# One block of scores for the second query block of the sliding attention, merged by a predicated copy

## The chip, the cores and the metric

The kernel runs on one core of a Trainium2 chip. The metric is the device time of one execution in microseconds, median over several runs. The core has TensorE (PE, with its weight loads PEld), VectorE (DVE), ScalarE (ACT), GpSimd (POOL) and SyncE (SP, which issues loads); each takes its own instructions in order.

## The reference

A decoder trunk of two layers over 256 tokens of width 1024. Each layer normalises the stream, projects it once, and feeds three token mixers: a Mamba-2 scan, a sliding-window attention with sinks, and a forgetting attention. Each is gated by SiLU, projected and merged. The sliding attention is what is touched:

```python
diff = qi + blk - sj
band = (diff >= 0) & (diff < SWA_WINDOW)
scores = jnp.where(mask[None, :, None, None], scores, -jnp.inf)
sink = jnp.broadcast_to(sinks..., scores.shape[:-1] + (1,))
probs = jax.nn.softmax(jnp.concatenate([scores, sink], axis=-1), axis=-1)[..., :-1]
out = jnp.einsum('bnkgqs,bnskd->bnqkgd', probs.astype(v.dtype), vb)
return out.reshape(b, s, SWA_HEADS * HEAD_DIM) * jax.nn.silu(z)
```

There are 16 query heads of 64 columns in four groups; a group shares its key and value head. Window and query block are both 128. So the first query block sees the lower triangle (with the diagonal) of key block 0; the second sees the strict upper triangle of key block 0 and the lower triangle of key block 1. A row of the second block has exactly 128 allowed keys among its 256 scores, and column j is allowed in one of the two key blocks and never in both.

## The kernel before

All tensors are float32. The large projections run as three fast matmuls on a high and a low part of both operands: weights arrive by SP into `raw`, ACT rounds them to `hi` (L291) and DVE subtracts for `lo` (L292). The projections are cut into units of 256 or 272 columns (`u_z`, `u_conv`, `u_cv`, `u_ck`, `u_cq`) and of 512 (`u_gate`, `u_proj`); they form the backbone of TensorE's stream, whose order is the order of the program.

Everything else is written as Python generators, and a planner puts their pieces between the units. `mm` and `transpose` advance a model clock, `launch` and each `yield` give a generator's next piece the earliest clock at which it may run, and `pump`, called at the end of a unit (and in the middle of a 512-column one), runs the pieces that are due, up to a budget. A yield of a number is a delay: `D_SOFT` = 7.0 from scores to transposes, `D_SOFT2` = 3.0 from the first group of transposes to the second, `D_EVAC` = 3.0 from there to giving back the token `pp`, of which there is one, so that attention quads follow one another. The order on DVE and ACT is chosen by the compiler's scheduler, mostly in the order in which the pieces are traced.

`swa_quad` handles one group of four heads (four quads a layer); `attn_quad` is the body that it shares with the forgetting attention (`fox_quad`). A quad works like this. `products` puts a head's scores into one PSUM bank of the pool `mx` (five banks; four are taken): columns 0 to 127 for the first query block, 128 to 383 for the second against both key blocks. L615 scales, adds the mask `wmask` and takes the row minimum of the negated scores with the sink, for 128 and for 256 columns, out to SBUF (`pp`). L621 exponentiates there with the row sum as a second output. Sinks are added to the sums (L625 to L628), L630 takes reciprocals, L633 scales `pp` in place, by a half of the reciprocal (the gate carries a factor of two). Then 12 transposes (three blocks of 128 columns for each head), four to a bank, and L652 copies each bank to SBUF on ACT. For key block 0 the transposed chances of both query blocks lie side by side, so the product with the values (`products_with_values`) takes 256 columns for key block 0 and 128 for key block 1. Values of two quads run together, ahead of the next quad's scores, and L676 multiplies them into the gate.

In the third quad's time the small matmuls of `decay_logits` (L749 to L760) need three `mx` banks of their own. Behind the fourth quad the scan's groups (`ssd_group`) start; they load `cumd` into buffers of the tag `L4` that the quads use too.

Of the kernel before, what the change touches and what calls it, by code (L numbers as in the profile page):

```python
# [13 lines left out]
AF = mybir.ActivationFunctionType  # L14
ALU = mybir.AluOpType

P = 128
S = 256
# [29 lines left out]
def hybrid_trunk(  # L48
# [5 lines left out]
    nc = tc.nc  # L54
# [45 lines left out]
    def mm(o, a, b, **kw):  # L100
        n = b.free_size()
        if a.dtype == F32R:
            clock["t"] += max(0.094, n / 2350.0)
        else:
            clock["t"] += max(0.2, n / 587.0) * (0.5 if a.free_size() == 64 or a.shape[0] == 32 else 1.0)
        nc.tensor.matmul(o, a, b, **kw)  # L106

    def transpose(o, a, i):
        clock["t"] += 0.109
        nc.tensor.transpose(o, a, i)  # L110
# [74 lines left out]
    for j in range(2):  # L185
        nc.sync.dma_start(x0[:, 0, j * 512:(j + 1) * 512], x2[0:P, j * 512:(j + 1) * 512])
    ident = T("ident", [P, P])
    make_identity(nc, ident)
    tri = T("tri", [P, P])
    nc.gpsimd.memset(tri, 1.0)  # L190
    nc.gpsimd.affine_select(out=tri, in_=tri, compare_op=ALU.is_ge, fill=0.0, base=0,
                            pattern=[[1, P]], channel_multiplier=-1)
# [3 lines left out]
                            pattern=[[1, P]], channel_multiplier=-1)  # L196
# [8 lines left out]
    nc.gpsimd.affine_select(out=wmask[:, P:2 * P], in_=wmask[:, P:2 * P],  # L205
                            compare_op=ALU.is_ge, fill=NEG, base=0,
                            pattern=[[-1, P]], channel_multiplier=1)
    nc.gpsimd.affine_select(out=wmask[:, 0:P], in_=wmask[:, 0:P],
                            compare_op=ALU.is_ge, fill=NEG, base=-1,
                            pattern=[[1, P]], channel_multiplier=-1)  # L210
    mhalf = T("mhalf", [P, 8])
    nc.gpsimd.memset(mhalf, -0.5)
    cs = T("cs", [P, 2, S])
# [125 lines left out]
    first, late = [], []  # L339
# [86 lines left out]
    for l in range(L):  # L426
        y = Layer()
# [156 lines left out]
            launch(1, swa_quad(y, g, q), D_Q)  # L584
        return rotated(y, done)

    def attn_quad(y, last, products, biases, nsink, v, vcols, sz, gated, scored=lambda: None):
# [15 lines left out]

        def score(p, i, b):
            return scs[2 * p + i][:, b * P:P + 2 * P * b]

        products(score)
        for p in range(2):
            pp = pps[p]
            ps_ = slice(4 * p, 4 * p + 4)  # L610
            ns = None if nsink is None else nsink(p)
            for i in range(2):
                for b, sl in blocks:
                    e = 4 * p + 2 * i + b
                    nc.vector.tensor_tensor_reduce(  # L615
                        out=pp[:, i, sl], in0=score(p, i, b), in1=biases(p, i, b), scale=-0.125,
                        scalar=1.0e30 if ns is None else ns[:, i:i + 1],
                        op0=ALU.add, op1=ALU.min, accum_out=nm[:, e:e + 1])
                for b, sl in blocks:
                    e = 4 * p + 2 * i + b  # L620
                    act(pp[:, i, sl], pp[:, i, sl], AF.Exp, scale=-1.0, bias=nm[:, e:e + 1],  # L621
                        accum_out=sums[:, e:e + 1])
            if nsink is not None:
                es = T("es", [P, 4], bufs=2)
                tt(es.rearrange("p (i b) -> p i b", i=2), nm[:, ps_].rearrange("p (i b) -> p i b", i=2),  # L625
                   bc(ns, 2, 2), op=ALU.subtract)
                act(es, es, AF.Exp)
                tt(sums[:, ps_], sums[:, ps_], es, op=ALU.add)  # L628
            rs = T("rsum", [P, 4], bufs=4)
            nc.vector.reciprocal(rs, sums[:, ps_])  # L630
            for i in range(2):
                for b, sl in blocks:
                    ts(pp[:, i, sl], pp[:, i, sl], rs[:, 2 * i + b:2 * i + b + 1], 0.5,  # L633
                       op0=ALU.mult, op1=ALU.mult)
        yield D_SOFT
        scored()

        order = [(0, 0), (0, 1), (1, 0), (1, 1), (0, 2), (1, 2),
                 (2, 0), (2, 1), (2, 2), (3, 0), (3, 1), (3, 2)]
        at = {hb: (n // 4, n % 4 * P) for n, hb in enumerate(order)}  # L640
        pTs = []
        for n, (h, b) in enumerate(order):
            if n == 6:
                yield D_SOFT2
            if n % 4 == 0:
                pt = pmx()
            transpose(pt[:, n % 4 * P:(n % 4 + 1) * P], pps[h // 2][:, h % 2, b * P:(b + 1) * P], ident)
            if n % 4 == 3:
                if n == 3:
                    two = T("L4", [P, 2, 512])  # L650
                pT = T("L2", [P, 512]) if n == 11 else two[:, n // 4, :]
                act(pT, pt, AF.Copy)  # L652
                pTs.append(pT)
        yield D_EVAC
        tokens["pp"] += 1

        def products_with_values(bank):
            py = bank()
            for p in range(2):
                for b, o in ((0, 0), (1, P)):  # L660
                    for i in range(2):
                        n, c = at[2 * p + i, 2 * b]
                        mm(py[64 * i:64 * i + 64, S * p + o:S * p + S], v[:, b, vcols(p, i)],
                           pTs[n][:, c:c + S - o], start=(b == 0), stop=(b == 1))
            return py


        pair.append((gated, products_with_values, sz))
        if len(pair) == 2:
            quads = pair[:]  # L670
            pair.clear()

            def values():
                for py, (_, _, own) in zip([f(bank) for (_, f, _), bank in zip(quads, (pmx, pmm))], quads):
                    o = own()
                    tt(o, py.rearrange("p (u s) -> p u s", u=2), o, op=ALU.mult)  # L676
            if not last:
                y.values.append(None)
            gates = lambda: all(g() for g, _, _ in quads)
            yield Half(gates) if last else gates  # L680
            if last:
                values()
            else:
                y.values[0] = values

    def swa_quad(y, g, q):
        yield lambda: 1 in y.sz

# [8 lines left out]
        yield from attn_quad(  # L697
            y, g == 3, products, lambda p, i, b: wmask[:, P:2 * P] if b == 0 else wmask,
            lambda p: y.nsink[:, 4 * g + 2 * p:4 * g + 2 * p + 2], y.bv,
            lambda p, i: slice(64 * g, 64 * g + 64),  # L700
            lambda: y.sz[1][:, 2 * g:2 * g + 2, :], lambda: (1, 2 * g + 1) in y.zdone)


    def logits(y, t, i, p):
# [494 lines left out]
    for y in layers:  # L1199
# [51 lines left out]
        if l == 0:  # L1251
            v, cv0, cv1 = cols(C_BV), cols(C_CV), cols(C_CV + 256)
# [8 lines left out]
        else:  # L1261
            cv0, v = cols(C_CV, 512), cols(C_BV)
# [43 lines left out]
        o = [sub([(0, w_out[l, :, c:c + n])], n) for c, n in ((0, 256), (256, 512), (768, 256))]  # L1306
# [43 lines left out]
    with tc.manual_schedule(engines={ENG.PE, ENG.DVE, ENG.Activation, ENG.Pool}):  # L1350
# [11 lines left out]
        p = pmx()  # L1362
# [93 lines left out]
        for i in range(2):  # L1456
# [57 lines left out]
```

## Time and profile before

| what | value |
|---|---|
| median of three runs | 820.61 us (819.9 to 821.44) |
| the profiled execution | 820.72 us, span 819.0 us |
| granted TensorE clock, mean | 0.999 |
| DMA | 170.35 MB, 208 GB/s on average |
| sliding stage, layer 0 | scores from 66.39 us, last values from 156.91 us |
| sliding stage, layer 1 | scores from 457.58 us, last values from 548.52 us |

Times in rows are microseconds from the start of the span unless marked ns. A row of the groups reads: line, engine, operation, output <- inputs, shape, count | busy us, mean ns of one | idle time before them and what ended it. A row of the chain reads: start, duration, what. A row of busy time by stretch reads: stretch, length, then busy time and count of PE, PEld, DVE, ACT, POOL, granted clock, DMA share, GB/s. A row of waits reads: engine, line <- who it waited for: total us, times, longest.

### The profile page before, as it was taken

The page shows a single profiled execution, that of the slowest core. Times are in us where ns is not written, and L with a number is a line of the kernel's source. Part 1 is how long each engine was busy: PE and PEld are TensorE (multiplying, and loading weights), DVE is VectorE, ACT ScalarE, POOL GpSimd, SP SyncE. Part 2 cuts the span into 40 slices and gives each one's busy share as a digit, 9 for nine tenths or more (in the row PEclk, how much of TensorE's full clock was granted, in tenths as well). Part 3 has the DMA queues.
Part 4 walks back from the last instruction along what each step waited for, and adds up shares of the span by engine and source line. Part 5 has one row for each costly group of instructions (what it writes and reads, how often), then busy time and mean ns, then how long its engine had stood idle before and what let it go on. Part 6 is the DMA issues. An engine that isn't in the chain of part 4 may idle for free.

```text
span 819.0 us, 15070 instructions
## 1 busy us (share of the span) xinstructions
PE 808.4 (99%) x5242; PEld 721.2 (88%) x5242; DVE 671.5 (82%) x1468; ACT 547.6 (67%) x1186; POOL 172.6 (21%) x232
## 2 busy tenths in 40 slices
PE   8999999999999999999999999999999999999996
PEld 8998988888888988888999898889888889888896
DVE  6879899888998787965786989988899878787665
ACT  7777878775776767543666777886567767684452
POOL 3066113130210001030005621314004210102100
PEclk9999999999999999999999999999999999999999
DMA  9897869797865554866689787869868565467632
GB/s 312 278 261 193 211 187 256 190 233 214 232 206 157 180 168 148 276 208 205 221 265 265 186 222 206 228 179 259 243 206 231 155 181 163 137 208 265 206 104 77
DMA packets 141653, 170.35 MB, mean 208 GB/s; under 512 B 9314, under 2 KB 110298, under 8 KB 141578
## 3 DMA queue, kind: packets, MB, share of 16 engines
q1 hardware_dynamic: 114960, 140.53, 54.8%
q0 software_dynamic: 12928, 12.63, 9.5%
q10 hardware_dynamic: 13690, 16.24, 6.5%
q8 instruction: 41, 0.67, 0.3%
q14 instruction: 34, 0.28, 0.1%
HBM read 154.63 MB, written 2.16 MB: 191 GB/s over the span
## 4 chain that ended last, share of the span: by engine, by line
PE 85%; DVE 4%; DMA 4%; ACT 4%; issue 2%; POOL 0%; SPq 0%; ACTq 0%; DVEq 0%; POOLq 0%
PE mm L106 75%; PE mx L106 7%; PE mx L110 3%; DMA L<-cumd 2%; DVE lo L292 1%; ACT hi L291 1%; DVE L L781 1%; ACT pp L621 1%; DMA L<-L 1%; DMA raw<-in_w_in_dram 1%; DMA bias<-cumd 1%; ACT L L778 0%; ACT L L490 0%; DVE L L830 0%; POOL bias L991 0%
## 5 line engine op out<-in xcount | busy, mean ns | idle before, releaser
L292 DVE TENSOR_TENSOR lo<-raw,hi 128x1024 fp32r<-128x1024 f32 (+2 forms) x276 | 310.5, 1144 | 53.2 <-ACT hi L291 50.5
L106 PE MATMUL mm<-L,hi 128*128 128x512 f32 x1056 | 353.2, 386 | 0.0
L106 PE MATMUL mm<-hi,L 128*128 128x512 f32 (+2 forms) x1232 | 323.3, 351 | 0.1
L291 ACT ACTIVATE hi<-raw 128x1024 fp32r<-128x1024 f32 (+2 forms) x276 | 263.9, 981 | 57.2 <-PE mm L106 45.2
L106 PE MATMUL mm<-L,lo 128*128 128x256 f32 x1056 | 266.6, 273 | 0.0
L106 PEld LDWEIGHTS mm<-hi,L 128*128 128x128 f32 x1232 | 216.9, 190 | 24.1 <-issue 1.3
L106 PEld LDWEIGHTS mm<-L,hi 128*128 128x128 f32 x1056 | 194.5, 190 | 26.4 <-issue 3.2
L106 PE MATMUL mm<-lo,L 128*128 128x512 f32 (+2 forms) x616 | 213.8, 349 | 1.8 <-DVE lo L292 1.8
L106 PEld LDWEIGHTS mm<-L,lo 128*128 128x128 f32 x1056 | 202.1, 191 | 5.5
L106 PEld LDWEIGHTS mm<-lo,L 128*128 128x128 f32 x616 | 116.3, 190 | 14.1 <-DVE lo L292 2.6
L492 POOL DMA_DIRECT2D L<-L x68 | 59.4, 925 | 184.5 <-ACT L L491 151.3
L621 ACT ACTIVATE pp<-pp,nm 128x128 f32<-128x128 f32 (+1 forms) x128 | 56.5, 442 | 30.8 <-DVE nm L615 30.7
L991 POOL TENSOR_SCALAR_AFFINE_SELECT bias<-bias 128x128 f32<-128x128 f32 x64 | 34.6, 592 | 93.5 <-DMA bias<-cumd 92.7
L781 DVE SCALAR_TENSOR_TENSOR L<-L,vec,L 128x255 f32<-128x255 f32 (+2 forms) x96 | 46.2, 481 | 2.2 <-ACT L L778 0.5
L490 ACT ACTIVATE L<-mm 128x256 f32<-128x256 f32 x84 | 31.6, 376 | 15.9 <-PE mm L106 14.2
L1025 ACT ACTIVATE L<-L 128x512 f32<-128x512 f32 x24 | 15.1, 629 | 31.6 <-DVE L L1022 27.2
L633 DVE TENSOR_SCALAR pp<-pp,rsum 128x128 f32<-128x128 f32 (+1 forms) x128 | 32.5, 319 | 0.5
L492 POOL DMA_DIRECT2D qt<-L x16 | 14.5, 990 | 81.9 <-ACT qt L491 40.4
L877 DVE SCALAR_TENSOR_TENSOR L<-L,L 128x256 f32<-128x256 f32 x48 | 21.4, 449 | 8.6 <-ACT L L876 8.3
L652 ACT ACTIVATE L<-mx 128x512 f32<-128x512 f32 x48 | 26.8, 595 | 1.5 <-PE mx L110 1.5
L1070 POOL TENSOR_TENSOR L<-L,L 128x512 f32<-128x512 f32 x8 | 12.8, 1598 | 68.4 <-DVE L L1069 68.4
L912 POOL TENSOR_TENSOR sm<-sm,mhalf 128x4 f32<-128x4 f32 x8 | 8.1, 1019 | 90.5 <-DVE sm L909 90.5
(197 smaller groups left out, 841.8 us busy)
## 6 DMA issues: line engine op xcount, KB each, us to landing
raw<-in_w_in_dram SPq DMA_DIRECT2D x191, 512.0 KB, 4.7
raw<-in_w_proj_dram SPq DMA_DIRECT2D x48, 512.0 KB, 5.3
L<-L POOLq DMA_DIRECT2D x72, 128.0 KB, 5.0
raw<-in_w_out_dram SPq DMA_DIRECT2D x16, 512.0 KB, 5.1
bias<-cumd ACTq DMA_DIRECT2D x16, 256.0 KB, 3.4
L<-cumd ACTq DMA_DIRECT2D x8, 512.0 KB, 5.9
L<-in_gate_bias_dram ACTq DMA_DIRECT2D x12, 256.0 KB, 5.9
qt<-L POOLq DMA_DIRECT2D x16, 128.0 KB, 5.6
```

The costliest lines, as they stand in the source:

```text
L106: nc.tensor.matmul(o, a, b, **kw)
L110: nc.tensor.transpose(o, a, i)
L291: keep(act)(hi, src, AF.Copy)
L292: keep(tt)(lo, src, hi.bitcast(F32), op=ALU.subtract)
L490: act(halves(lo), ordered(p[:, S:2 * S]), AF.Copy)
L492: nc.gpsimd.dma_start(out, lo, accum_op=ALU.add)
L621: act(pp[:, i, sl], pp[:, i, sl], AF.Exp, scale=-1.0, bias=nm[:, e:e + 1], accum_out=sums[:, e:e + 1])
L633: ts(pp[:, i, sl], pp[:, i, sl], rs[:, 2 * i + b:2 * i + b + 1], 0.5, op0=ALU.mult, op1=ALU.mult)
L652: act(pT, pt, AF.Copy)
L781: stt(a[:, s:S], x_[:, 0:S - s], y.vec[:, 16 * j + u:16 * j + u + 1], a[:, s:S], op0=ALU.mult, op1=ALU.add)
L877: stt(o, th, 1.0, o, op0=ALU.add, op1=ALU.mult)
L991: nc.gpsimd.affine_select(out=bias[:, i, dst], in_=bias[:, i, src], compare_op=ALU.is_ge, fill=NEG, base=0, pattern=[[-1, P]], channel_mul ...
```

## The change

Only the sliding attention is changed; the forgetting attention keeps its path behind `window=False`. The first query block of each head goes through L615 as before. For the second, `copy_predicated` writes the scores of key block 0 over those of key block 1 wherever the lower-triangle mask is not zero, inside PSUM; a reduction takes the maximum of the merged 128 columns, a small combination turns two heads' maxima into biases with the sink, and the exponential reads the merged scores from PSUM. `pp` now holds query block 0 of the four heads in one buffer and query block 1 in the other, sums are kept by query block, and one multiplication of 4 x 128 columns scales each. Eight transposes remain. The bank of query block 0 is copied on ACT; that of query block 1 is evicted twice on DVE, once times the mask `other` (key block 0's part) and once times `tri` (key block 1's). The factor of a half moves into the product with the gate. The delay between scores and transposes is `D_FOLD` = 8.0.

```diff
+D_FOLD = 8.0
-    wmask = T("wmask", [P, 2 * P])
+    wmask, other = T("wmask", [P, P]), T("other", [P, P])
...
+        for h in range(4) if window else ():
+            own = pps[0][:, h // 2, h % 2 * P:h % 2 * P + P]
+            nc.vector.tensor_tensor_reduce(
+                out=own, in0=scs[h][:, 0:P], in1=wmask, scale=-0.125, scalar=nsink[:, h:h + 1],
+                op0=ALU.add, op1=ALU.min, accum_out=nm[:, h:h + 1])
+            chances(h, 0, own)
+        for h in range(4) if window else ():
+            own = scs[h][:, 2 * P:3 * P]
+            nc.vector.copy_predicated(own, wmask.bitcast(mybir.dt.uint32), scs[h][:, P:2 * P])
+            nc.vector.tensor_reduce(nm[:, 4 + h:5 + h], own, axis=mybir.AxisListType.X, op=ALU.max)
+            if h % 2 == 1:
+                hs = slice(h - 1, h + 1)
+                nh = slice(3 + h, 5 + h)
+                stt(nm[:, nh], nm[:, nh], -0.125, nsink[:, hs], op0=ALU.mult, op1=ALU.min)
+                for i in (h - 1, h):
+                    chances(i, 1, scs[i][:, 2 * P:3 * P])
+        for b in range(2) if window else ():
+            hs = slice(4 * b, 4 * b + 4)
+            es = T("es", [P, 4], bufs=2)
+            tt(es, nm[:, hs], nsink, op=ALU.subtract)
+            act(es, es, AF.Exp)
+            tt(sums[:, hs], sums[:, hs], es, op=ALU.add)
+            rs = T("rsum", [P, 4], bufs=4)
+            nc.vector.reciprocal(rs, sums[:, hs])
+            tt(of_heads(b), of_heads(b), bc(rs.rearrange("p (i j) -> p i j", i=2), 3, P), op=ALU.mult)
...
-        yield D_SOFT
+        yield D_FOLD if window else D_SOFT
...
+            first, both = T("L4", [P, 2, 512]), T("L2", [P, 512])
+            for b in range(2):
+                if b == 1:
+                    yield D_SOFT2
                 pt = pmx()
+                for h in range(4):
+                    transpose(pt[:, h * P:(h + 1) * P], pps[b][:, h // 2, h % 2 * P:h % 2 * P + P], ident)
+                ptv = pt.rearrange("p (h q) -> p h q", h=4)
+                if b == 0:
+                    act(first[:, 0, :], pt, AF.Copy)
+                else:
+                    tt(first[:, 1, :].rearrange("p (h q) -> p h q", h=4), ptv, bc(other, 1, 4), op=ALU.mult)
+                    tt(both.rearrange("p (h q) -> p h q", h=4), ptv, bc(tri, 1, 4), op=ALU.mult)
...
+                    if window:
+                        stt(o, po, 0.5, o, op0=ALU.mult, op1=ALU.mult)
```

More of the change, by code (lines that the diff above doesn't have):

```diff
@@ L201, in hybrid_trunk @@
     ones = onesr.bitcast(F32)
-    wmask = T("wmask", [P, 2 * P])
+    wmask, other = T("wmask", [P, P]), T("other", [P, P])
     nc.gpsimd.memset(wmask, 0.0)
-    nc.gpsimd.affine_select(out=wmask[:, P:2 * P], in_=wmask[:, P:2 * P],
-                            compare_op=ALU.is_ge, fill=NEG, base=0,
+    nc.gpsimd.affine_select(out=wmask, in_=wmask, compare_op=ALU.is_ge, fill=NEG, base=0,
                             pattern=[[-1, P]], channel_multiplier=1)
-    nc.gpsimd.affine_select(out=wmask[:, 0:P], in_=wmask[:, 0:P],
-                            compare_op=ALU.is_ge, fill=NEG, base=-1,
-                            pattern=[[1, P]], channel_multiplier=-1)
+    nc.gpsimd.memset(other, 1.0)
+    nc.gpsimd.affine_select(out=other, in_=other, compare_op=ALU.is_ge, fill=0.0, base=-1,
+                            pattern=[[-1, P]], channel_multiplier=1)
     mhalf = T("mhalf", [P, 8])
@@ L585, in u_bq, with attn_quad @@
         return rotated(y, done)
-    def attn_quad(y, last, products, biases, nsink, v, vcols, sz, gated, scored=lambda: None):
+    def attn_quad(y, last, products, biases, nsink, v, vcols, sz, gated, scored=lambda: None, window=False):
         yield Half("pp")
@@ L607, in attn_quad, with of_heads, chances @@
         products(score)
-        for p in range(2):
+        def of_heads(b):
+            return pps[b].rearrange("p i (j q) -> p i j q", j=3)[:, :, 0:2, :]
+        def chances(h, b, of):
+            e = 4 * b + h
+            act(pps[b][:, h // 2, h % 2 * P:h % 2 * P + P], of, AF.Exp, scale=0.125 if b else -1.0,
+                bias=nm[:, e:e + 1], accum_out=sums[:, e:e + 1])
+        for h in range(4) if window else ():
[23 more added lines that the diff above has]
+            tt(of_heads(b), of_heads(b), bc(rs.rearrange("p (i j) -> p i j", i=2), 3, P), op=ALU.mult)
+        for p in () if window else range(2):
             pp = pps[p]
             ps_ = slice(4 * p, 4 * p + 4)
-            ns = None if nsink is None else nsink(p)
             for i in range(2):
@@ L616, in attn_quad @@
                         out=pp[:, i, sl], in0=score(p, i, b), in1=biases(p, i, b), scale=-0.125,
-                        scalar=1.0e30 if ns is None else ns[:, i:i + 1],
+                        scalar=1.0e30,
                         op0=ALU.add, op1=ALU.min, accum_out=nm[:, e:e + 1])
@@ L622, in attn_quad @@
                         accum_out=sums[:, e:e + 1])
[L623 to L628, printed above, removed]
             rs = T("rsum", [P, 4], bufs=4)
@@ L634, in attn_quad @@
                        op0=ALU.mult, op1=ALU.mult)
-        yield D_SOFT
+        yield D_FOLD if window else D_SOFT
         scored()
[L638 to L645, printed above, removed]
-                pt = pmx()
[L647 to L653, printed above, removed]
+        if window:
[3 more added lines that the diff above has]
+                    yield D_SOFT2
+                pt = pmx()
+                for h in range(4):
[6 more added lines that the diff above has]
+                    tt(both.rearrange("p (h q) -> p h q", h=4), ptv, bc(tri, 1, 4), op=ALU.mult)
+        else:
+            order = [(0, 0), (0, 1), (1, 0), (1, 1), (0, 2), (1, 2),
+                     (2, 0), (2, 1), (2, 2), (3, 0), (3, 1), (3, 2)]
+            at = {hb: (n // 4, n % 4 * P) for n, hb in enumerate(order)}
+            pTs = []
+            for n, (h, b) in enumerate(order):
+                if n == 6:
+                    yield D_SOFT2
+                if n % 4 == 0:
+                    pt = pmx()
+                transpose(pt[:, n % 4 * P:(n % 4 + 1) * P], pps[h // 2][:, h % 2, b * P:(b + 1) * P], ident)
+                if n % 4 == 3:
+                    if n == 3:
+                        two = T("L4", [P, 2, 512])
+                    pT = T("L2", [P, 512]) if n == 11 else two[:, n // 4, :]
+                    act(pT, pt, AF.Copy)
+                    pTs.append(pT)
@@ L661, in products_with_values @@
                     for i in range(2):
-                        n, c = at[2 * p + i, 2 * b]
-                        mm(py[64 * i:64 * i + 64, S * p + o:S * p + S], v[:, b, vcols(p, i)],
-                           pTs[n][:, c:c + S - o], start=(b == 0), stop=(b == 1))
+                        h = 2 * p + i
+                        if window:
+                            m = both[:, h * P:(h + 1) * P] if b else first[:, :, h * P:(h + 1) * P]
+                        else:
+                            n, c = at[h, 2 * b]
+                            m = pTs[n][:, c:c + S - o]
+                        mm(py[64 * i:64 * i + 64, S * p + o:S * p + S], v[:, b, vcols(p, i)], m,
+                           start=(b == 0), stop=(b == 1))
             return py
@@ L675, in values @@
                     o = own()
-                    tt(o, py.rearrange("p (u s) -> p u s", u=2), o, op=ALU.mult)
+                    po = py.rearrange("p (u s) -> p u s", u=2)
+                    if window:
+                        stt(o, po, 0.5, o, op0=ALU.mult, op1=ALU.mult)
+                    else:
+                        tt(o, po, o, op=ALU.mult)
             if not last:
@@ L697, in swa_quad @@
         yield from attn_quad(
-            y, g == 3, products, lambda p, i, b: wmask[:, P:2 * P] if b == 0 else wmask,
-            lambda p: y.nsink[:, 4 * g + 2 * p:4 * g + 2 * p + 2], y.bv,
+            y, g == 3, products, None, y.nsink[:, 4 * g:4 * g + 4], y.bv,
             lambda p, i: slice(64 * g, 64 * g + 64),
-            lambda: y.sz[1][:, 2 * g:2 * g + 2, :], lambda: (1, 2 * g + 1) in y.zdone)
+            lambda: y.sz[1][:, 2 * g:2 * g + 2, :], lambda: (1, 2 * g + 1) in y.zdone, window=True)
     def logits(y, t, i, p):
```

## The prediction

> **What bounds the kernel now.** I read the page first, then busy time by stretch for the two stages of the sliding attention (one per layer), then who TensorE waited for.
>
> ```profile
> span 819.0 us, 15070 instructions
> ...
> PE 808.4 (99%) x5242; PEld 721.2 (88%) x5242; DVE 671.5 (82%) x1468; ACT 547.6 (67%) x1186; POOL 172.6 (21%) x232
> ```
> ```profile
> 62.00:160.00 98.00, 98.00 (x746) 87.48 (x745) 88.98 (x239) 78.93 (x209) 30.54 (x36) 1.00 0.77 204
> ...
> 454.00:552.00 98.00, 97.82 (x744) 87.06 (x743) 89.20 (x240) 78.08 (x209) 29.69 (x35) 1.00 0.76 202
> ```
> ```profile
> PE mm L106 <- DVE lo L292: 1.2, 1, 1.2
> ...
> PE mm L106 <- DVE lo L292: 0.6, 1, 0.6
> ...
> PEld mx L106 <- DVE nm L615: 0.6, 2, 0.3
> ```
>
> TensorE is the bound: 808.4 of 819.0 us. In the stretches after the colon (length, then PE, PEld, DVE, ACT, POOL busy, granted clock 1.00) it is busy for 98.00 of 98.00 us and 97.82 of 98.00 us, while DVE has some 9 us of slack in each and ACT some 19. The waits that count here are few: 1.2 us (layer 0) and 0.6 us (layer 1) for split weights just behind the sliding attention, and 0.6 us of layer 1 inside it, for L615. So an instruction taken from TensorE is worth its own time, and one added to DVE costs nothing until something on TensorE finds it late.
>
> **TensorE: the term of the sum.** A quad (four heads) issues 12 transposes now, 8 afterwards; the products with keys and with values keep their number and shapes. Four quads in two layers: 4 x 8 = 32 transposes go.
>
> ```profile
> L110 PE MATMUL mx<-ident,pp 128*128 128x128 f32 x192 | 26.3, 273 | 0.0
> ```
> ```profile
> 66.39 1.52 PE mx L106 x32
> 67.92 8.06 PE mm L106 x48
> 75.97 0.66 PE mx L110 x6
> 76.63 5.24 PE mm L106 x32
> ```
>
> The mean of one is 273 ns, but they overlap: on the chain of waits six of them take 0.66 us, 0.11 us each. 32 x 0.11 = **-3.5 us**. The Trainium skill (TensorE: Matmul & The Clock Gate, Part 4: PE-mode transpose) gives about 275 ns for one inside a kernel; by that figure alone the saving would be an estimate of 8.8 us. The row's mean agrees with it, the chain does not charge it, and the chain decides.
>
> **DVE and ACT: what moves.** Per quad, from these rows:
>
> ```profile
> L633 DVE TENSOR_SCALAR pp<-pp,rsum 128x256 f32<-128x256 f32 x64 | 22.5, 352 | 0.0
> ...
> L633 DVE TENSOR_SCALAR pp<-pp,rsum 128x128 f32<-128x128 f32 x64 | 18.4, 287 | 0.5
> L830 DVE SCALAR_TENSOR_TENSOR L<-L,acum,negtri 128x128 f32<-128x128 f32 x64 | 17.6, 347 | 0.0
> ...
> L845 DVE TENSOR_TENSOR L<-L,mx 128x512 f32<-128x512 f32 x24 | 15.3, 681 | 0.0
> L615 DVE CUSTOM_DVE_ANT_0 pp<-mx,wmask,nsink 128x256 f32<-128x256 f32 x32 | 15.2, 476 | 0.0
> ...
> L615 DVE CUSTOM_DVE_ANT_0 pp<-mx,wmask,nsink 128x128 f32<-128x128 f32 x32 | 11.0, 343 | 0.0
> L615 DVE DVE_READ_ACCUMULATOR2_ANT nm<- 128x1 f32 x128 | 10.4, 82 | 0.0
> ```
> ```profile
> L621 ACT ACTIVATE pp<-pp,nm 128x256 f32<-128x256 f32 x64 | 31.7, 495 | 0.2 <-DVE nm L615 0.2
> ...
> L652 ACT ACTIVATE L<-mx 128x512 f32<-128x512 f32 x48 | 26.8, 595 | 1.5 <-PE mx L110 1.5
> ...
> L621 ACT ACTIVATE pp<-pp,nm 128x128 f32<-128x128 f32 x64 | 24.9, 390 | 30.5 <-DVE nm L615 30.5
> ```
>
> DVE before: 4 x 476 + 4 x 343 + 8 x 82 + 4 x 352 + 4 x 287 = 6.49 us. After: 4 x (343 + 82) for the first block; four predicated copies and four reductions of 128 columns, which no row shows; two normalisations of 128x512 and two masked evictions of 128x512 at 681 each; two small combinations at 0.16 us (L625 in the rows of DVE further down). For copy and reduction the bounds are 287 ns (L633, 128 columns) and 476 ns (L615, 256 columns); I take 347, the elementwise row of two inputs at the same 128 columns. Sum 1.70 + 8 x 0.347 + 4 x 0.681 + 0.32 = 7.52 us: **+1.0 us a quad** (+0.6 to +2.1), +4 us in a stage where DVE is busy for 89 of 98. That is covered by the idle 9 us, on average only. The stages of exponent sums and reciprocals stay two of each a quad and cancel; the product with the gate is one 128x512 instruction before and after. The Trainium skill (VectorE: DVE Perf Modes, The TRN2 errata) prices a fp32 two-input instruction at (N+151)/0.96 ns. By that the copy and the reduction would be an estimate of 291 ns each and the quad +0.6 us; at 512 columns it says 691 where the trace has 681, so the low half of my bounds is likelier.
>
> ACT: 4 x 495 + 4 x 390 + 3 x 595 = 5.33 us before; 8 x 390 + 595 = 3.72 after: -1.6 us a quad. ACT is not the bound; nothing is counted for it. The mask setup on POOL trades one fill of 256 columns and two selects for two fills and two selects of 128, before TensorE needs any of it: nothing.
>
> **The order of the work.** The kernel's own planner runs pending stages at the end of a unit of the input projection. A unit of 16 matmuls is 8 x (512+256)/2350 = 2.61 on its clock, and two take 5.24 us on the chain, so clock and trace agree. The first quad's scores end at 67.92, three units (7.84) pass the delay of 7.0, and the transposes follow. With a delay of 8.0 that is a fourth unit: 10.46. Walking the four quads through the units: the first and the fourth wait one unit longer, the second finds 2.61 + 2.78 + 2.78 = 8.17 (two of its units have 272 columns, 24 x 272/2350) and the third 2.61 + 1.49 + 2 x 2.61 = 9.3 (1.49 is the clock of the small matmuls of `decay_logits`), as long as before. So the last values of the stage come two units (5.2 us) later against the stream of projections. That costs TensorE nothing in itself. It matters in two places.
>
> **Place one: banks of scores.** The second block's exponentials now read PSUM on ACT, so a head's bank is held until ACT is done with it, where L615 used to let go. In the third quad three more banks are needed at once, one unit behind the scores (the cumulative sums of `decay_logits`), from a pool of five of which four hold scores. Layer 1 shows it today:
>
> ```profile
> 503.73 1.59 PE L106 MATMUL mx<-L,qt 32*128 32x128 f32 x32
> 507.97 0.52 PE L106 MATMUL mx<-da,tri 128*128 128x16 f32 x4
> 508.60 0.61 PE L106 MATMUL mx<-tri,da 128*16 128x128 f32 x4
> ```
> ```profile
> 507.79 0.34 DVE L615 CUSTOM_DVE_ANT_0 pp<-mx,wmask,nsink 128x128 f32<-128x128 f32 x1
> ...
> 508.06 0.48 DVE L615 CUSTOM_DVE_ANT_0 pp<-mx,wmask,nsink 128x256 f32<-128x256 f32 x1
> ...
> 510.79 0.16 DVE L625 TENSOR_TENSOR es<-nm,nsink 128x4 f32<-128x4 f32 x1
> ```
> ```profile
> 508.18 0.40 ACT L621 ACTIVATE pp<-pp,nm 128x128 f32<-128x128 f32 x1 [4.91 <-DVE nm L615]
> ```
> ```profile
> 68.58 0.34 DVE L615 CUSTOM_DVE_ANT_0 pp<-mx,wmask,nsink 128x128 f32<-128x128 f32 x1
> ```
>
> The second matmul group starts at 508.60, just after the first head's second L615 ends at 508.54. Afterwards that head is free only behind four L615 at a pitch of 0.27 (508.06 - 507.79), two copies and two reductions at about 0.30, a small combination of 0.16, a hand-over of 0.12 and an exponential of 0.39: some 2.95 us after DVE starts, where it was 0.75. TensorE asks about 3.1 us after the scores end (a unit and the first group). How long it waits hangs on when DVE starts: 2.5 us after the scores' end here (505.32 to 507.79), 0.7 us in the first quad (67.92 to 68.58). At 2.5 the wait is 2.3 us a layer, at 0.7 it is 0.5. The late start belongs to the long chain of small logits, which will be four more microseconds ahead of the scores, so I take 1.2: about 1.05 a layer. Two layers, less the 0.6 paid already: **+1.5 us** (+0.4 to +4.0). Behind this stand the projections that follow on TensorE, so it is paid in full.
>
> **Place two: behind the stage.**
>
> ```profile
> 156.91 1.45 PE mx L106 x16
> ...
> 159.47 8.88 DMA L<-cumd
> ...
> 168.58 4.83 DMA bias<-cumd
> ```
>
> Loads of `cumd` take the buffers (`L4`) that the last values leave, DVE and ACT stop in their order for them, and the split weights behind them come 1.2 and 0.6 us late. With values two units later this shifts by 2.6 to 5.2 us against the projections, but the scan group that follows shifts too and its 128-column work then lies behind the weights. I take nothing; bounds -1.8 (both waits go) to +10.5 (5.2 a layer).
>
> **The sum.** 820.72 (the profiled execution: 819.0 span and 1.7 around it) - 3.5 + 1.5 = 818.7; that execution lies 0.1 above the median of 820.61, so **818.6 us**, 0.25% faster.
>
> **The rivals.**
> - *The whole gain, and the small waits go too* (12%): DVE is early, the bank is free in time, the waits behind the stage vanish: 820.6 - 3.5 = 817.1, down to 815.3. For it: ACT gives up 6.5 us a stage. Against it: DVE carries more.
> - *The bank takes it all* (10%): DVE starts as late as in layer 1 today, +3.5 to +4.0: 820.6 to 821.1. For it: the 0.6 us row. This is also how the change might not do what it says: the transposes go and the time stays.
> - *The chain behind the stage decides, and it is slower* (26%): values two units late, the loads of 8.88 and 4.83 us follow them one behind the other, and weights for the next projection are late by one unit more in each layer: 818.6 + 2 x 2.6 = 823.8; by two units, 829.1. It decides from the point where the loads leave less than a unit before the branch projection. For it: there is no slack there now, TensorE waits already. Against it: the scan's DVE work is put back as well.
> - *DVE runs out* (8%): if copy and reduction cost 476 ns, a quad has +2.1 us, DVE is at 97 of 98, and the transposes of the second quad, whose delay has only 0.17 to spare, wait; about a microsecond a quad, 818.6 + 8 = 826.6.
>
> **How the numbers follow.** My forecast has 44%, between 816.9 and 820. A measurement of this kernel tells about 0.2% (1.6 us) from no change; four points of the forecast's 44 fall inside it. Faster: 40 + 12 = 52%. Same: 4 + 10 = 14%. Slower: 26 + 8 = 34%. The range starts at 815.3 and goes to 825.0, which takes in the one-unit case and leaves out the two-unit case and most of DVE's; some 16% lie outside. The likeliest case alone has 816.9 to 820.
>
> **What would show it.** Right: 160 transposes from `pp` in place of 192; sliding quads with eight in two groups of four; TensorE's busy time down by some 3.5 us; a wait of a matmul in `mx` for ACT of about a microsecond a layer in the third quad; 10.5 us from scores to transposes in the first and fourth. Wrong: TensorE idle for several microseconds behind the stage on split weights (the slower rival), a transpose that waits for DVE (DVE has run out), or a copy or reduction of more than 0.5 us.

## The result and the profile after

The changed kernel takes **827.0 us** (826.69 to 827.98), the kernel before 820.66: a ratio of 1.0079, 95% interval 1.0062 to 1.0097. It is 6.3 us slower; 818.6 was forecast, and the range ended at 825.0. The profiled execution took 827.98 us, with a span of 826.2.

The page of the changed kernel, its span and the busy time of the engines:

```profile
span 826.2 us, 14993 instructions
...
PE 810.0 (98%) x5210; PEld 720.9 (87%) x5210; DVE 676.6 (82%) x1452; ACT 540.7 (65%) x1170; POOL 161.4 (20%) x233
```

TensorE has 32 matmuls fewer (5242 to 5210) and yet 1.6 us more of busy time. Something made its instructions longer, and idle time was added as well. Who TensorE waited for (us in total, times, longest):

```profile
PE mx L107 <- ACT pp L614: 7.6, 2, 3.8
```

Beside this row only waits at the kernel's beginning are left; the 1.8 us for split weights behind the stage are gone. One wait of 3.8 us stands in each layer, at the third quad. This is its place in layer 0, in the timeline (start, duration; in brackets the idle time ahead of it and what ended it), first TensorE, then VectorE, then ScalarE:

```profile
114.91 1.59 PE L107 MATMUL mx<-L,qt 32*128 32x128 f32 x32
...
119.16 0.51 PE L107 MATMUL mx<-da,tri 128*128 128x16 f32 x4
123.48 1.04 PE L107 MATMUL mx<-tri,da 128*16 128x128 f32 x4 [3.81 <-ACT pp L614]
```
```profile
117.11 0.18 DVE L796 TENSOR_TENSOR da<-dt,nega 128x32 f32<-128x32 f32 x1
...
117.61 0.68 DVE L727 SCALAR_TENSOR_TENSOR L<-mx,L 128x512 f32<-128x512 f32 x1
118.21 0.47 DVE L833 SCALAR_TENSOR_TENSOR L<-L,vec,L 128x253 f32<-128x253 f32 x1
118.60 0.68 DVE L727 SCALAR_TENSOR_TENSOR L<-mm,L 128x512 f32<-128x512 f32 x1
119.20 1.21 DVE L292 TENSOR_TENSOR lo<-raw,hi 128x1024 fp32r<-128x1024 f32 x1
120.33 0.34 DVE L619 CUSTOM_DVE_ANT_0 pp<-mx,wmask,nsink 128x128 f32<-128x128 f32 x1
```
```profile
122.97 0.37 ACT L614 ACTIVATE pp<-mx,nm 128x128 f32<-128x128 f32 x1 [0.40 <-DVE nm L632]
```

The scores of the third quad end at 116.50 (114.91 and 1.59). VectorE starts on them at 120.33, 3.8 us later, and it was never idle in between. The chain of small logits, which was to set this start, ends with L796 at 117.29. Behind it two taps of the convolution (L833), two products of the quads before with their gates (L727) and a split of weights (L292) still stand ahead in the queue, 3.0 us in all. In layer 1 of the kernel before, where the scores end at 505.32, the chain ends with L744 at 507.27 and one product is left ahead of L615 at 507.79:

```profile
507.08 0.19 DVE L744 TENSOR_TENSOR da<-dt,nega 128x32 f32<-128x32 f32 x1
507.19 0.68 DVE L676 TENSOR_TENSOR L<-mm,L 128x512 f32<-128x512 f32 x1
```

So the chain did come earlier against the scores, 0.8 us behind them and not 1.95, and VectorE came later. The first head's exponential from PSUM begins 2.64 us after VectorE has started, at 122.97, and the matmul that needs that head's bank begins at 123.48, right behind it.

What follows on TensorE runs slowly. Busy time by stretch (length, then PE, PEld, DVE, ACT, POOL, then the granted clock):

```profile
123.00:126.00 3.00, 2.52 (x11) 1.61 (x12) 2.69 (x12) 3.00 (x16) 0.49 (x1) 0.50 0.19 66
126.00:129.00 3.00, 3.00 (x10) 2.64 (x11) 1.71 (x5) 0.88 (x5) 0.37 (x1) 0.50 0.30 44
129.00:130.00 1.00, 1.00 (x5) 0.82 (x5) 0.21 (x1) 0.75 (x1) 0.00 (x0) 0.61 0.14 33
...
519.00:522.00 3.00, 3.00 (x14) 2.06 (x13) 2.76 (x9) 2.87 (x14) 0.87 (x1) 0.50 0.03 5
522.00:523.00 1.00, 1.00 (x6) 0.89 (x6) 0.93 (x3) 0.00 (x0) 0.00 (x0) 0.84 0.87 127
```

The clock was halved. Length times what is missing from 1.00 is 1.5 + 1.5 + 0.39 = 3.4 us lost in layer 0, so 6.8 us at half clock, and 1.5 + 0.16 = 1.7 us lost in layer 1, so 3.4 us at half clock. That is 5.1 us together. In layer 0 the half clock begins at 122.96 by the trace's record of the clock, 0.5 us ahead of the matmul that ends the stand, so some 0.25 us of this are idle time already and 4.9 us come on top of the stands.

The groups of instructions (busy us, mean ns of one):

```profile
L111 PE MATMUL mx<-ident,pp 128*128 128x128 f32 x160 | 22.8, 273 | 0.0
...
L643 DVE TENSOR_TENSOR pp<-pp,rsum 128x512 f32<-128x512 f32 x16 | 10.9, 690 | 0.3
L627 DVE COPY_PREDICATED mx<-wmask,mx 128x128 f32<-128x128 uint32 x32 | 8.5, 289 | 0.3
L628 DVE TENSOR_REDUCE nm<-mx 128x1 f32<-128x128 f32 x32 | 8.4, 284 | 0.0
...
L679 DVE TENSOR_TENSOR L<-mx,other 128x512 f32<-128x512 f32 x8 | 5.5, 683 | 0.0
```

**An account of the span.** Expected and there: -3.5 (160 transposes, not 192). Gone: -1.8 (split weights behind the stage) and -0.2 (the old wait for a bank: its row of 0.6 us in the prediction is one of weight loads, and the matmuls themselves stood for 98.00 - 97.82 = 0.18 us in that stretch). New: +7.6 (the two stands) and +4.9 (half clock). Together +7.0; the span grew by 7.2.

### The profile page after: what moved, and what is told of

Its sections match the earlier page's. It is cut to its first block, busy times and chain, and to the rows that moved or that the text cites. A ratio compares the mean times of both kernels' runs of the same rounds, so it can differ in the third digit from the quotient of the medians.

```text
span 826.2 us, 14993 instructions
## 1 busy us (share of the span) xinstructions
PE 810.0 (98%) x5210; PEld 720.9 (87%) x5210; DVE 676.6 (82%) x1452; ACT 540.7 (65%) x1170; POOL 161.4 (20%) x233
## 4 chain that ended last, share of the span: by engine, by line
PE 87%; DVE 7%; issue 2%; ACT 2%; DMA 1%; POOL 0%; SPq 0%; ACTq 0%; POOLq 0%; DVEq 0%
PE mm L107 78%; PE mx L107 7%; PE mx L111 3%; DVE lo L292 2%; DVE L L833 2%; DMA raw<-in_w_in_dram 1%; ACT pp L614 1%; ACT hi L291 0%; DVE pp L619 0%; DVE pp L643 0%; DVE L L784 0%; POOL sm L258 0%; DVE mx L627 0%; DVE L L1216 0%; DVE L L727 0%
## 5 line engine op out<-in xcount | busy, mean ns | idle before, releaser
L292 DVE TENSOR_TENSOR lo<-raw,hi 128x1024 fp32r<-128x1024 f32 (+2 forms) x276 | 312.4, 1150 | 55.2 <-ACT hi L291 52.4
L490 ACT ACTIVATE L<-mm 128x256 f32<-128x256 f32 x84 | 31.9, 379 | 26.2 <-PE mm L107 22.0
L833 DVE SCALAR_TENSOR_TENSOR L<-L,vec,L 128x255 f32<-128x255 f32 (+2 forms) x96 | 46.1, 480 | 1.8 <-ACT L L830 0.2
L1043 POOL TENSOR_SCALAR_AFFINE_SELECT bias<-bias 128x128 f32<-128x128 f32 x64 | 26.3, 446 | 86.3 <-DMA bias<-cumd 86.2
L656 ACT ACTIVATE pp<-pp,nm 128x128 f32<-128x128 f32 x64 | 28.2, 441 | 9.9 <-DVE nm L650 9.9
L614 ACT ACTIVATE pp<-pp,nm 128x128 f32<-128x128 f32 x32 | 12.6, 394 | 25.4 <-DVE nm L619 24.6
L964 POOL TENSOR_TENSOR sm<-sm,mhalf 128x4 f32<-128x4 f32 x8 | 9.9, 1242 | 88.0 <-DVE sm L961 88.0
L491 ACT ACTIVATE L<-mm 128x256 f32<-128x256 f32 x68 | 25.9, 381 | 0.7 <-DMA L<-L 0.6
L928 ACT ACTIVATE L<-L 128x256 f32<-128x256 f32 x48 | 19.8, 413 | 9.9 <-DVE L L483 9.7
```

The source lines that it names most:

```text
L292: keep(tt)(lo, src, hi.bitcast(F32), op=ALU.subtract)
L490: act(halves(lo), ordered(p[:, S:2 * S]), AF.Copy)
L491: last = act(halves(out), ordered(p[:, 0:S]), AF.Copy)
L614: act(pps[b][:, h // 2, h % 2 * P:h % 2 * P + P], of, AF.Exp, scale=0.125 if b else -1.0, bias=nm[:, e:e + 1], accum_out=sums[:, e:e + 1])
L833: stt(a[:, s:S], x_[:, 0:S - s], y.vec[:, 16 * j + u:16 * j + u + 1], a[:, s:S], op0=ALU.mult, op1=ALU.add)
L928: act(th, o, AF.Tanh, scale=0.5)
```

## The experiments

The theory after the result: the loss is the stand of TensorE at the scores' banks and the half clock behind it, both due to VectorE's late start in the third quad. Its rivals: the planner's order (the delay of 8.0) makes the loss, or the chain behind the stage does. Medians of the kernel before were 821.83, 821.82, 821.41 and 821.40 us in the four groups of runs below, so runs of different groups are compared by their ratios to it.

**The sums two units later.** In the changed kernel:

```diff
-D_GN1, D_GN2, D_CUM, D_H, D_M = 8.0, 13.5, 12.0, (4.8, 6.4), 5.0
+D_GN1, D_GN2, D_CUM, D_H, D_M = 8.0, 13.5, 22.5, (4.8, 6.4), 5.0
```

> The changed kernel with the delay of the cumulative sums (D_CUM) at 22.5 in place of 12.0, so that their three banks are asked for three units behind the third quad's scores and not one. Theory BANK (TensorE stands 3.8 us a layer because the exponentials on ACT hold the banks of scores, and its clock halves behind each stand): no wait of a matmul in mx for L614, granted clock 0.999 as before, 827.0 - 7.6 - 5 = 814 to 815 us. Rival LOAD (the added DVE work is what is late, and the bank is only where it shows): TensorE waits elsewhere in the stage for DVE, the time stays above 820 us.

Measured: 830.13 us, ratio 1.0100 (1.0083 to 1.0118). The stands and the half clock are gone, but TensorE now waits at the end of the stage and behind it, and the 814 to 815 expected did not come. Its longest waits:

```profile
PE mx L107 <- DVE L L897: 2.8, 4, 1.3
PE mm L107 <- DVE lo L292: 2.7, 2, 2.3
PE mm L107 <- DVE rsum L642: 2.0, 2, 1.2
```

What was meant to take one wait away brought others (9.7 us with the rows below 1.5 us). This run alone could mean that the stand merely hid a chain behind the stage, or that late sums are costly by themselves.

**The same in the kernel before**, the same one constant.

> The kernel before with D_CUM at 22.5 in place of 12.0, to see what the moved sums do by themselves. Theory BANK: only the 0.6 us of layer 1 goes, 820 us (819.5 to 821). Rival: moving the sums helps for a reason that has nothing to do with the change, and the kernel before gains more than 2 us as well.

Measured: 823.32 us, ratio 1.0025 (1.0015 to 1.0034). Late sums cost something without the change too, where 819.5 to 821 was expected: 3.3 us of waits for split weights (L292) in place of 1.8.

**The old delay.** In the changed kernel:

```diff
-D_FOLD = 8.0
+D_FOLD = 7.0
```

> The changed kernel with D_FOLD at 7.0, so that the quads stand against the projections as in the kernel before. Theory BANK: the banks are held on ACT all the same, only DVE starts earlier (some 2 to 2.5 us behind the scores instead of 3.9): a wait of 1.8 to 2.3 us a layer, 820 to 821 us if the clock stays up, up to 825 if it halves again. Rival ORDER (the longer delay and the new places of the pieces are at fault): no wait in mx, 815 to 817 us.

Measured: 828.88 us, ratio 1.0089 (1.0071 to 1.0107). The order of the stages was not the loss. The stand is 2.8 us here, with VectorE 2.8 us behind the scores (114.08 to 116.87). The time is above the 825 expected at most, and the waits for split weights, 2.8 us, are back. Its row of the wait, and its stretches around the two stands:

```profile
PE mx L107 <- ACT pp L614: 5.5, 2, 2.8
```
```profile
115.00:130.00 15.00, 12.03 (x68) 10.24 (x67) 13.16 (x46) 10.42 (x35) 1.95 (x3) 0.89 0.58 157
510.00:525.00 15.00, 12.03 (x71) 9.79 (x64) 13.17 (x47) 9.23 (x31) 1.74 (x2) 0.89 0.58 152
```

0.11 of 15 us is missing from the clock in each, 1.65 us, so some 3.3 us at half clock behind a stand of 2.8.

**The bank let go by VectorE.** The merged scores go to SBUF through the instruction that the first block uses, with a block of zeros (`none`) as its mask, and the exponentials read SBUF as before the change:

```diff
-            nc.vector.tensor_reduce(nm[:, 4 + h:5 + h], own, axis=mybir.AxisListType.X, op=ALU.max)
...
+            nc.vector.tensor_tensor_reduce(
+                out=to, in0=own, in1=none, scale=-0.125, scalar=nsink[:, h:h + 1],
+                op0=ALU.add, op1=ALU.min, accum_out=nm[:, 4 + h:5 + h])
+            chances(h, 1, to)
```

> The changed kernel, but the merged scores go through L615's kind of instruction (scale, minimum with the sink, out to SBUF) in place of the reduction and the small combination, so that DVE and not ACT lets go of the bank. Theory BANK: the first head's bank is free some 1.4 us after DVE starts in place of 3, the wait falls from 3.8 to some 2.2 us a layer, 819 to 824 us, by whether the clock still halves. Rival LOAD: DVE has slightly more to do, so the time is that of the changed kernel or above it.

Measured: 824.37 us, ratio 1.0032 (1.0021 to 1.0042). Its wait row and stretches:

```profile
PE mx L107 <- DVE nm L631: 5.5, 2, 2.7
```
```profile
115.00:130.00 15.00, 12.26 (x87) 9.93 (x80) 14.25 (x49) 8.60 (x31) 1.72 (x2) 0.89 0.57 167
510.00:525.00 15.00, 12.27 (x62) 10.09 (x61) 13.00 (x44) 9.12 (x33) 1.74 (x2) 0.77 0.52 142
```

Without the exponential in the bank's chain the stand is 2.7 us instead of 3.8. Most of it stays, since VectorE starts no earlier (4.3 us behind the scores, 116.05 to 120.32), and the clock still falls.

**One bank for the sums.** The three sums go into different places of one bank and are read out after the last of them, so they need no bank that holds scores. Their place in the order is the changed kernel's:

```diff
         pa = pmx()
+        pr, pf = pa[0:16, 32:32 + S], pa[64:80, 32:32 + S]
...
-        pr = pmx()
...
-        pf = pmx()
```

> The three cumulative sums of the gates go into one bank of PSUM, written one after another and read out afterwards, at the place that the changed kernel gives them; nothing else is changed. They need no bank that the third quad's scores hold. If the stand at the third quad and the half clock behind it are the whole loss (7.6 us of waiting and some 5 us of half clock), the time is 827 - 12.7 = about 814 to 815. If what the late-sums run showed (waits behind the stage of the matmuls for VectorE, 8 to 10 us over both layers) comes whenever the stand is gone, because the stand is what lets VectorE catch up, the time is 822 to 826 with no half clock in mid-run. If those waits came only because the sums were late, it is near 816. The row of matmuls in mx for the exponentials goes in all cases.

Measured: **817.96 us**, ratio 0.9957 (0.9943 to 0.9972). The page and the waits:

```profile
span 816.7 us, 14993 instructions
...
PE 806.1 (99%) x5210; PEld 718.1 (88%) x5210; DVE 675.5 (83%) x1452; ACT 538.7 (66%) x1170; POOL 167.0 (20%) x233
```
```profile
PE mx L107 <- DVE L L896: 1.6, 4, 1.1
...
PE mm L107 <- DVE L L1073: 0.4, 2, 0.2
```

No stand, no half clock, and only 2.0 us of waits behind the stage. The chain behind the stage was not waiting its turn behind the stand; the first run's new waits came with the lateness of its sums.

**The same bank in the kernel before.**

> The same one bank for the cumulative sums in the kernel before. Its row of a matmul in mx behind the scores' banks was 0.6 us over the run; if the bank is worth no more than this row there, the time is 819.5 to 820.7 beside 820.7. If one bank by itself does something else (a later read-out, later loads of the sums), the same amount shows here and has to be taken off the run with the change.

Measured: 821.35 us, ratio 0.9997 (0.9983 to 1.0011): nothing. Its busy time on the page:

```profile
PE 808.9 (99%) x5242; PEld 721.4 (88%) x5242; DVE 671.7 (82%) x1468; ACT 546.5 (67%) x1186; POOL 170.5 (21%) x232
```

Between these two kernels only the change under study differs, and neither has the stand: 821.35 - 817.96 = 3.4 us, of which TensorE's busy time accounts for 808.9 - 806.1 = 2.8. That is the change by itself, its longer delay included.

**The stand filled with work.** In the changed kernel, 32 transposes that nobody reads, behind the first sum:

```diff
             mm(pa[:, 16 * c:16 * c + 16], tri, da[:, c, :], start=True, stop=True)
+        for _ in range(32):
+            nc.tensor.transpose(pa[:, 2 * P:3 * P], ident, ident)
```

> In the changed kernel 32 transposes of a constant, which nobody reads, are put on TensorE between the first cumulative sum and the two that wait for the scores' banks: 32 x 0.11 = 3.5 us of work in each layer, in a stand of 3.8 us. The wait remains, filled with work. If the half clock follows from the stand, the wait falls to about 0.3 us a layer, the two stretches of half clock go, and the time falls by the 5.1 us that they lost: 821 to 823. If the half clock has another cause (power, a fixed point of the program), the stretches stay and the time is 826 to 828. If the transposes last longer than the stand, the time is 827 plus the excess.

Measured: 822.75 us, ratio 1.0013 (1.0003 to 1.0022). The timeline of layer 0 and the stretches around both places:

```profile
119.02 3.69 PE L803 MATMUL mx<-ident 128*128 128x128 f32 x32
122.99 0.61 PE L107 MATMUL mx<-tri,da 128*16 128x128 f32 x4 [0.28 <-ACT pp L614]
```
```profile
115.00:130.00 15.00, 14.72 (x123) 13.15 (x116) 14.03 (x46) 8.79 (x32) 1.72 (x2) 1.00 0.58 168
510.00:525.00 15.00, 14.73 (x107) 13.41 (x106) 12.76 (x39) 11.19 (x37) 3.43 (x6) 1.00 0.54 140
```

The bank comes as late as it did, TensorE does 7.4 us of useless work, and the kernel is 4.3 us faster (827.0 to 822.75; by the ratios 1.0079 - 1.0013, 5.4). So the half clock is a price of its own on top of the wait, and it follows from TensorE having no work in the stand.

**The sums one unit later.** The first experiment's constant at 20.0 in place of 22.5.

> In the changed kernel the cumulative sums are due 8 us later, which puts them one unit of projections (2.6 us) behind their old place, half as far as in the late-sums run; the three banks stay. The wait for the scores' banks should shrink by the unit, from 3.8 to about 1.2 us a layer, too short to halve the clock if a stand of 2.3 us did not. Were this all, the time is 827 - 5.1 - 5.2 = 816.7. If what the late-sums run lost behind the stage grows with the lateness of the sums (about 10 us there for two units, none with one bank at the old place), one unit gives back some 3 to 5 us of it: 820 to 822, with waits of TensorE for VectorE behind the stage. If the late-sums run lost it by another cause, there are no such waits and the time is near 817.

Measured: 821.01 us, ratio 0.9995 (0.9983 to 1.0007). Its waits:

```profile
PE mx L107 <- ACT pp L614: 2.4, 2, 1.2
...
PE mx L107 <- DVE L L897: 1.4, 3, 1.0
```

The stand is shorter by the unit (2.6), 3.8 to 1.2, and 1.2 us leave the clock alone. The waits behind the stage are 2.1 us (0.7 more for L1074), about as with one bank, so one unit of lateness cost nothing there. The 820 to 822 came out, but by the stands that were left, not by waits behind the stage. Two units cost some 8 us of waits (9.7 in the first run, 2.0 with one bank); which piece of the chain turns between the two was not followed up.

**One bank and the old delay.** The one-bank kernel with D_FOLD at 7.0.

> One bank for the sums and, with it, the planner's delay between scores and transposes back at 7 us in place of 8, so that the stages keep the units they had before the change. If the longer delay of the change costs anything by itself, this is faster than 818.0, by up to 1 us. If the transposes now come before the softmax is done (scores to transposes are 10.5 us in the changed kernel's first quad, one unit less here), TensorE waits at the transposes for VectorE and the time is 818 to 822.

Measured: 822.57 us, ratio 1.0009 (0.9997 to 1.0021). TensorE waits 2.8 us for split weights (L292) and 1.8 us at the transposes for VectorE (L640). The longer delay of the change is worth some 4.3 us by the ratios (1.0009 - 0.9957) once the stand is gone.

**The masks on GpSimd.** In the changed kernel:

```diff
-                    tt(first[:, 1, :].rearrange("p (h q) -> p h q", h=4), ptv, bc(other, 1, 4), op=ALU.mult)
-                    tt(both.rearrange("p (h q) -> p h q", h=4), ptv, bc(tri, 1, 4), op=ALU.mult)
+                    act(first[:, 1, :], pt, AF.Copy)
+                    fv = first[:, 1, :].rearrange("p (h q) -> p h q", h=4)
+                    gtt(both.rearrange("p (h q) -> p h q", h=4), fv, bc(tri, 1, 4), op=ALU.mult)
+                    gtt(fv, fv, bc(other, 1, 4), op=ALU.mult)
```

> In the changed kernel the two masked evictions of the second block (0.68 us each on VectorE) become one plain copy on ScalarE and two multiplications from SBUF on GpSimd. If VectorE begins the third quad's softmax late because these evictions of the quad before stand ahead of it in the queue, it begins 1.3 us earlier, the stand at the scores' banks is about 2.5 us a layer in place of 3.8, and the time falls by 2.6 us, and by up to 5.1 us more if a stand of 2.5 us is short enough to leave the clock alone: 819 to 825. If the queue ahead is filled by other work that takes their place (splits of weights, taps), VectorE begins as late as before and the time is 826 to 828. If GpSimd's multiplications come out late, the products with the values wait for GpSimd.

Measured: 837.07 us, ratio 1.0180 (1.0155 to 1.0204), above all that was expected. The stand grew to 4.9 us, and TensorE waits 3.2 us for GpSimd's products. VectorE starts 5.8 us after the scores' end. Why, the timeline shows, GpSimd first, then VectorE:

```profile
110.12 1.61 POOL L681 TENSOR_TENSOR L<-L,tri 128x512 f32<-128x512 f32 x1
111.81 1.36 POOL L682 TENSOR_TENSOR L<-L,other 128x512 f32<-128x512 f32 x1
```
```profile
109.58 0.48 DVE L835 SCALAR_TENSOR_TENSOR L<-L,vec,L 128x254 f32<-128x254 f32 x1
...
110.11 1.92 DVE L835 SCALAR_TENSOR_TENSOR L<-L,vec,L 128x253 f32<-128x253 f32 x1
111.94 1.30 DVE L786 SCALAR_TENSOR_TENSOR L<-L 128x64 f32<-128x64 f32 x1
```

The tap takes 1.92 us instead of 0.48 and the small instruction 1.30 instead of 0.22: each ends about when an instruction of GpSimd does. VectorE won 1.3 us and lost 2.5 (the same two long rows stand in layer 1). A further split of weights then came ahead of the softmax. So it was not tried cleanly whether less work on VectorE alone starts it earlier.

**One bank and the masks on GpSimd.**

> The same move with the one bank for the sums, where nothing waits for the scores' banks. The run with one bank alone has 1.6 us of waits for VectorE behind the stage over both layers; less work on VectorE can take away at most these: 816.5 to 818. Slower than 818.5 if GpSimd's multiplications or the loads that GpSimd issues behind them are late.

Measured: 832.65 us, ratio 1.0128 (1.0102 to 1.0154), by the ratios 14 us above one bank alone. There is no wait for the scores' banks; TensorE waits 4.0 us for VectorE (L1075), 1.9 us for GpSimd (L682) and 3.4 us at the transposes. One of the two waits for L1075 in the timeline, and a stretch behind it:

```profile
157.37 0.45 PE L107 MATMUL mm<-L,hi 128*128 128x512 f32 x1 [1.99 <-DVE L L1075]
```
```profile
158.00:160.00 2.00, 2.00 (x9) 1.70 (x8) 1.80 (x4) 1.41 (x4) 0.78 (x1) 0.58 1.03 329
```

Here a stand of 2.0 us, at another place, was followed by half clock; so was the other one, in layer 1.

## Why the prediction was wrong, step by step

- **TensorE, -3.5 us: right.** The pair with one bank measures 3.4 us (2.8 in TensorE's busy time, the rest in waits), far from the 8.8 us that the mean of 273 ns would give. The pitch on the chain, 0.11 us, told what a transpose costs.
- **DVE, +1.0 us a quad: right, at the lower bound.** Copy 289 ns and reduction 284 ns, where 347 was taken; with the evictions at 683 and the normalisation at 690 the quad is 1.70 + 8 x 0.287 + 4 x 0.687 + 0.32 = 7.06 us, +0.6. VectorE did not run out, so the fourth rival falls.
- **The order: right.** On the chain of waits the first and the fourth quad have 10.68 and 10.59 us of projections between scores and transposes, 10.46 by the planner's clock. "Costs TensorE nothing in itself" held too.
- **Place one is the step that failed**: the mechanism, the quad and the waiting matmul were named, but "so I take 1.2" for VectorE's start behind the scores was 3.8. The prediction's own chain, 2.3 us of wait at a start of 2.5, gives 3.6 at 3.8, and 3.8 was measured. The start at 2.5 in layer 1 of the kernel before was the nearest row, and even that was too early. It was argued down because the chain of small logits would be four microseconds earlier. It came 0.6 us (layer 0) and 1.15 us (layer 1) nearer to the scores' end, and it is only one piece of a queue that was full: 3.0 us of taps, gate products and a split stood behind it, where one product of 0.5 us had stood. The range of the term, +0.4 to +4.0, ended at the latest start seen before. And what was paid already was 0.2 us of TensorE's time, not 0.6, so the term came to 7.6 - 0.2 = +7.4.
- **A term was missing**: half clock follows the stand, +4.9 us. No row of before has a stand this long in the middle of the kernel, and the sum took a wait at its length alone.
- **Place two, 0: right for the change alone** (2.0 us of waits behind the stage with one bank, where the kernel before has 1.8), and -1.8 in the changed kernel. That VectorE catches up there while TensorE stands is argued; the filled stand, which gives it the same time, has no such waits either.
- With these sizes the forecast's own sum is 818.7 + 5.9 + 4.9 - 1.8 = 827.7, beside 827.98 of the profiled run.
- **The rivals.** "The bank takes it all" had the right place, with +3.5 to +4.0 where +7.4 was paid, and without the clock. The slower rival had the sign and the wrong place: nothing waits behind the stage. That 827.0 lies near the 826.6 of the rival "DVE runs out" is chance: its premise, 476 ns for copy and reduction, did not hold.

The change is a gain spoilt by one resource at one place. The version with one bank for the sums keeps it: 0.9957 of the kernel before, the fastest of the runs here.

## What to carry to other kernels

When a buffer is held longer, price the wait from the latest start that its releasing engine shows anywhere, and read what stands in that engine's queue; an engine that is busy nine tenths of a stage does not start early because one piece of its work has moved. Price a stand of TensorE twice, as idle time and, from some 2 us here, as slow time after it. If the holder can't be made faster, look for a user that can do without: three small results in one bank were worth 9 us here (827.0 to 818.0; 10 by the ratios), and nothing in the kernel before.

## What the runs showed of the hardware

**The clock behind a stand.** All stands of 2.7 us and more in the middle of a run (up to 4.9, two in each of four kernels) were followed by half clock; both of 2.0 us in the last run were, one of 2.3 us was not (the L292 row of the late-sums run, in the stretch below, at a clock of 1.00), and work that nobody reads prevented it. The slow time does not follow the length of the stand: after 3.8 us it was 6.8 in layer 0 and 3.4 in layer 1. The Trainium skill (TensorE: Matmul & The Clock Gate, Part 1: The HAM clock gate) says that activity is judged in free-running windows of 3.413 us, and the trace agrees: slow stretches of one to three such windows (3.41, 6.83 and 10.24 us), and in the changed kernel's record of the clock 116.05 us at full clock up to the first of them, 34 windows. Its advice there, no idle gaps above about 3.4 us, does not reach far enough by these runs, where 2.0 us were followed by half clock.

So where a stand falls in the windows may count beside its length, which would explain the 2.0 and the 2.3. Counted by such windows from the first full clock in each run's record, the stand of 2.0 us (155.38 to 157.37) lies whole in one window, 154.90 to 158.31, and the half clock begins at its end; the stand of 2.3 us (193.49 to 195.79) is divided by an edge at 194.21 into 0.7 and 1.6. No run varied the phase alone, so this is not shown.

```profile
165.00:205.00 40.00, 35.56 (x213) 29.80 (x208) 31.36 (x55) 20.94 (x38) 8.46 (x10) 1.00 0.83 229
```

**VectorE beside GpSimd.** Two instructions of VectorE with two inputs in SBUF, issued beside GpSimd's tensor instructions, ended only about when these did (1.92 us for 0.48, 1.30 for 0.22). The Trainium skill (SBUF — State Buffer, Who interferes with whom) describes it: such an instruction contends with one of GpSimd that reads SBUF, for a pair of ports that the two share and that one holds for a whole instruction while the other waits. The rows above agree.
